# Two gate products called earlier, one lead for PSUM banks and operands in the planner, a new table of shifts and a new order of the first loads, in a float32 encoder block

## The chip, the cores and the metric

The kernel runs on one core of one Trainium2 chip. The metric is the device time of one execution in microseconds (us), lower is better; a kernel is timed in several runs and the median is given. TensorE is called PE here, VectorE DVE, ScalarE ACT, GpSimd POOL and the engine that issues most DMAs SP, as in the profile.

## What is computed

One layer of an encoder on 512 real tokens and 16 meta tokens of width 1024. The input is normalised, projected once, and goes through two attention mixers side by side; their results are gated per channel, merged and projected, and a gated feed-forward net follows. Cut to what matters:

```python
u = rms_norm(h, pre_mix_gain)
qa, ka, va, qb, kb, vb, g = split(u @ w_in)
o_swa  = windowed_gqa_sink_attention(rope(qa), rope(ka), va, sink)   # 16 heads, band of 3 blocks + meta keys
o_diff = differential_attention(rope(qb), rope(kb), vb, lam)         # 8 heads, two softmaxes each, dense
gates  = sigmoid(g + b_gate)                                         # 2 x 1024 channels
merged = gates[:, :1024] * (o_swa @ w_branch_swa) + gates[:, 1024:] * (o_diff @ w_branch_diff)
h = h + rms_norm(merged @ w_out)
f = (silu(u2 @ w_gate) * (u2 @ w_up)) @ w_ffn_out                    # u2 = rms_norm(h)
out = h + rms_norm(f)
```

All is float32 in and out. A product of two float32 matrices is made of three matmuls on operands that are split into a rounded high part and a remaining low part (fp32r): high by high, high by low, low by high. So each weight and each activation needs a copy (the high part, on ACT) and a subtraction (the low part, on DVE or POOL) before PE can use it.

## The kernel before

Everything lies transposed: channels on the 128 partitions, tokens along the row. The stages are, in order of time:

1. **Start.** The transposed input is loaded in eight tiles of 128 channels (`x_load`, L412 to L415, on SP) and split into `xh` on ACT (L419) and `xl` on DVE (L420). The weights of the first key projection come in four pieces between them (`k_weights`, L425 to L432). The line that lists the order is L434: `x0 w0 x1 x2 w1 x3 x4 w2 x5 x6 w3 x7`. The piece `w0` is loaded and split in two halves, for the channel tiles 0 and 1. PE runs 41 small matmuls on zeros first (L402), then L474: for each channel tile twelve matmuls, high weight by `xh`, high weight by `xl`, low weight by `xh`. DVE, ACT, SP and PE run in the order in which the code stands there.
2. **Planned stretch** (about 20 to 500 us). From `v_swa` to the second last stage every step is not issued at once but handed to a planner, `Plan` (L117 to L256). A step has an engine, a duration, what it reads and writes, and a priority. `Plan.run` then plays the steps through with these durations: for each engine it looks which steps have their operands and a free buffer, and takes the one with the lowest due time (on PE the priority alone; on the others the ready time plus a slack). The order found that way is the order in which the instructions are issued, and on the chip each engine keeps to it. A step that waits for an operand from another engine is ready a lag after that (`lag`, L138: 0.27 us to PE, 0.036 to 0.092 us to ACT, DVE and POOL). A step that needs a fresh buffer or PSUM bank is ready 0.05 us after the bank was left, on all engines (L219). `SHIFT` (L127) is a table of numbers that moves the due time of single steps by hand.
3. What is planned: keys, values and queries of the banded attention (`k_swa`, `v_swa`, `q_swa`), its 16 blocks (`s_swa`: scores `Sw` L763 on two banks, mask and minimum on DVE L767, exponential on ACT L771, scaling on POOL L778; `t_swa`: transposes `tr` L813, split into `ah` and `al`, products into the one bank `O` L820), the first eight gate products (`gate`), the differential attention (`qk`, `vd`, `s_diff` with scores `Sd` L912 in one double bank, `t_diff` with `Od` L981 and L983), the branch products `b1`, the second eight gate products (`gate2`), and of the branch product `w_bd` the first two column tiles, but for their last step in the sum. Products into the three banks `pr` are what PE does between the steps of the attentions.
4. **After the plan.** The gates `z2` get their tanh on ACT (L1113), the last step of the two `w_bd` tiles is made, then the other six, the output projection, and the feed-forward net, none of which the change touches.

The seam between plan and rest matters here. The last head ends in `t_diff(7)`: its sum of squares on PE (`mp`, L995 and L996), then on ACT `v` (L999), logarithm and exponential (L1004, L1005) and a square (L1006), three steps on DVE (L1007, L1009, L1011), the high part `dh` on ACT (L1018) and the low part `dl` on DVE (L274). The last step (k = 7) of every `w_bd` tile reads that `dh` and `dl`. The eight tanhs stand behind the plan in the code and are tied only to the last exponential (L1005); a scheduler of the framework places them among ACT's last steps.

In the program of before the gate products are called in this order: gates 0 and 1 ahead of the blocks, gates 2, 3, 4 and 5 behind blocks 0, 1, 2 and 8 (line L1062), gates 6 and 7 behind `qk(0)`.

Of the kernel before, what the change touches and what calls it, by code (L numbers as in the profile page):

```python
# [22 lines left out]
KT = D // P  # L23
# [93 lines left out]
class Plan:  # L117
# [9 lines left out]
    SHIFT = (  # L127
# [8 lines left out]

# [56 lines left out]
    def run(self):  # L193
# [4 lines left out]
        while any(todo.values()):  # L198
            best = None
            for e, ks in todo.items():  # L200
                cand = []
                for k in ks:
# [11 lines left out]
                    for tag, n in need.items():  # L214
                        f = sorted(x for x in self.slots[tag] if x is not None)
                        if len(f) < n:
                            t = None
                            break
                        t = max(t, f[n - 1] + 0.05)  # L219
                    if t is None:  # L220
# [38 lines left out]
def encoder(ctx, tc, I, out, dbg=None):  # L259
# [165 lines left out]
    def k_weights(i):  # L425
        if i % 2 == 0:
            wK.append([wp.tile([P, 4, 2, P], dt, tag=t, name=t, bufs=RB) for t, dt in (("wr", F32), ("wh", F32R), ("wl", F32R))])
        w = [t[:, 2 * (i % 2):2 * (i % 2) + 2] for t in wK[-1]]
        src = I["w_k"][i].rearrange("p (k a c) -> p k a c", k=2, a=2)
        for ks in (slice(0, 1), slice(1, 2)) if i == 0 else (slice(0, 2),):  # L430
            sp.dma_start(out=w[0][:, ks], in_=src[:, ks])
            split(w[1][:, ks], w[2][:, ks], w[0][:, ks])  # L432

    for what in ("x0", "w0", "x1", "x2", "w1", "x3", "x4", "w2", "x5", "x6", "w3", "x7"):  # L434
        n = int(what[1])
        if what[0] == "w":
            k_weights(n)
        else:
            x_load(n)
            x_split(n)  # L440
# [110 lines left out]
    def weights(src, dep=()):  # L551
# [5 lines left out]
        e, eng, xfer = ("ACT", act, 2.0) if nfill[0] > 3 else ("SP", sp, 0.0)  # L557
        T(e, 0.38, lambda: eng.dma_start(out=wr.t, in_=src.rearrange("p (k c) -> p k c", k=KT)), w=[wr], dep=dep,
          prio=pr_, land=0.7, xfer=xfer)
        T("ACT", 1.05, lambda: act.copy(out=wh.t, in_=wr.t), r=[wr], w=[wh], prio=pr_)  # L560
        if nfill[0] % 2:
            parts = []
            for q in range(4):
                ks = slice(2 * q, 2 * q + 2)
                parts.append(T("POOL", 0.69, lambda ks=ks: sub_hi(wl.t[:, ks], wr.t[:, ks], wh.t[:, ks], pool), r=[wr, wh],
                               keep=[wl], prio=pr_))
        else:
            parts = [T("DVE", 1.23, lambda: sub_hi(wl.t, wr.t, wh.t), r=[wr, wh], keep=[wl], prio=pr_, port=True)] * 4
# [43 lines left out]
    def move(out, in_, r, w, xfer, dep=()):  # L612
        return T("SP", 0.64, lambda: sp.dma_start(out=out().bitcast(F32), in_=in_().bitcast(F32)), r=r, w=w, dep=dep,
                 prio=2, xfer=xfer)
# [83 lines left out]
    def keys(n):  # L698
        K = buf("kk")
        K.mk = lambda: KP[(K.slot + 1) % 4][:, :, 0:n]  # L700
        return K
# [81 lines left out]
    def t_swa(u):  # L783
# [24 lines left out]
        for n, (o, kb) in enumerate(keys):  # L808
            tr = bank("tr", 2, "tr")

            def trans(o=o, tr=tr):
                for hh in range(4):
                    pe.transpose(out=tr.t[:, hh * P:(hh + 1) * P], in_=pt.t[:, hh, o:o + P], identity=ident)  # L813
            Ttr[u].append(T("PE", 0.355, trans, r=ph, w=[tr], keep=[pt], prio=0, chain="tr", land=0.08))
            ah, al = sb("ah", [P, 512], F32R, "ah", 2), sb("al", [P, 512], F32R, "al", 2)
# [79 lines left out]
    def s_diff(h):  # L895
# [9 lines left out]
        for c in range(2):  # L905
            for i in range(4):
# [16 lines left out]
                if c:  # L923
                    T("ACT", 0.2, lambda one=one: act.activation(out=den.t[:, 1, one], in_=den.t[:, 1, one], func=AF.Copy,
                                                                 scale=ilam), w=pw, on=["lam"], prio=0)
# [30 lines left out]
    def t_diff(h):  # L956
# [4 lines left out]
        for kb in range(5):  # L961
# [4 lines left out]
            def trans(o=o, kk=kk, tr=tr):  # L966
                for i in range(4):
                    pe.transpose(out=tr.t[0:kk, i * P:(i + 1) * P], in_=a[i]()[:, o:o + kk], identity=ident)  # L968
            T("PE", 0.355, trans, r=A, w=[tr], keep=hd["keep"], prio=0, chain="tr", land=0.08)
            if kb == 4:  # L970
# [86 lines left out]
    for u in range(16):  # L1057
        s_swa(u)
        t_swa(u)
        if u in (1, 5):  # L1060
            q_swa(2 + u // 4)
        for j in {0: (2,), 1: (3,), 2: (4,), 8: (5,)}.get(u, ()):  # L1062
            gate(j)
# [4 lines left out]
    qk(0)  # L1068
    for j in (6, 7):
        gate(j)  # L1070
    vd(0)
# [600 lines left out]
```

## Time and profile before

| what | us |
|---|---|
| median of three runs | 942.48 (941.61 to 942.53) |
| the profiled execution | 942.37 |
| its span, first to last instruction | 940.6 |
| PE busy | 928.5 |
| DVE, ACT, POOL busy | 714.9, 534.7, 253.5 |

The profiled execution took 942.37 us, 1.8 us of it outside the span of the instructions. PE has 5,852 matmuls. A matmul's record lasts longer than the distance to the next one: one of 512 columns is recorded with 0.39 us while the next starts about 0.23 us later, since they are pipelined and their ends are modelled. So PE can be shown as busy while it waits for up to some 0.16 us, and short waits are to be read from the distance of the starts. The granted clock of PE is 1.00 in every stretch up to 920 us.

### The profile page before, as it was taken

What the parts mean: (1) busy time and instruction counts of PE and PEld (TensorE: products, weight loads), DVE (VectorE), ACT (ScalarE), POOL (GpSimd) and SP (SyncE); (2) the same over time, 40 slices, a digit from 0 to 9 for tenths busy, and PEclk for the clock granted to TensorE, in tenths of its full rate; (3) what the DMA queues carried; (4) which work ended last, traced back from release to release, by engine and by line L of the source; (5) the groups of instructions that cost most, each with busy time, mean ns of one, the idle gap of its engine ahead of it and who ended that gap; (6) DMA issues with size and microseconds to landing.
All of it is one profiled execution on the core that took longest, in us unless ns stands there. A gap on an engine that the chain in (4) does not pass through costs nothing.

```text
span 940.6 us, 15671 instructions
## 1 busy us (share of the span) xinstructions
PE 928.5 (99%) x5852; PEld 831.9 (88%) x5852; DVE 714.9 (76%) x1194; ACT 534.7 (57%) x997; POOL 253.5 (27%) x320
## 2 busy tenths in 40 slices
PE   9999999999999999999999999999999999999996
PEld 9878878898898999999788888998999999988885
DVE  5847799997675767888664866876888888699975
ACT  6427677765565457667556433754555555555541
POOL 2645555564243333255032411500000000000000
PEclk9999999999999999999999999999999999999999
DMA  9564131216414333335332560364333333180122
GB/s 329 170 168 136 49 95 43 71 38 183 119 38 133 92 93 111 81 102 136 102 134 67 181 201 24 118 195 138 111 91 113 113 90 113 49 332 23 46 68 90
DMA packets 38012, 107.75 MB, mean 115 GB/s; under 512 B 6176, under 2 KB 7200, under 8 KB 37936
## 3 DMA queue, kind: packets, MB, share of 16 engines
q1 hardware_dynamic: 29872, 77.78, 27.7%
q10 hardware_dynamic: 8064, 28.97, 9.9%
q8 instruction: 46, 0.75, 0.3%
q14 instruction: 30, 0.25, 0.1%
HBM read 88.09 MB, written 2.10 MB: 96 GB/s over the span
## 4 chain that ended last, share of the span: by engine, by line
PE 88%; DVE 6%; ACT 2%; DMA 2%; issue 1%; SPq 0%; ACTq 0%; DVEq 0%
PE pr L308 20%; PE pr L310 20%; PE pr L309 20%; PE Sd L912 3%; PE wk L309 2%; PE wk L308 2%; PE wk L310 2%; PE tr L968 2%; PE O L820 2%; PE tr L310 1%; PE tr L308 1%; PE tr L309 1%; PE Od L981 1%; PE tr L813 1%; PE Sw L763 1%; DVE p L767 1%
## 5 line engine op out<-in xcount | busy, mean ns | idle before, releaser
L308 PE MATMUL pr<-xh,wh 128*128 128x264 f32 (+1 forms) x592 | 192.9, 326 | 0.4 <-DVE tb L585 0.2
L309 PE MATMUL pr<-xl,wh 128*128 128x264 f32 (+1 forms) x592 | 189.4, 320 | 0.0
L310 PE MATMUL pr<-xh,wl 128*128 128x264 f32 (+1 forms) x592 | 189.3, 320 | 0.0
L274 POOL TENSOR_TENSOR wl<-wr,wh 128x256 fp32r<-128x256 f32 (+1 forms) x130 | 126.8, 999 | 131.5 <-ACT wh L560 65.4
L308 PEld LDWEIGHTS pr<-xh,wh 128*128 128x128 f32 x592 | 111.4, 188 | 8.4 <-issue 0.5
L310 PEld LDWEIGHTS pr<-xh,wl 128*128 128x128 f32 x592 | 111.4, 188 | 8.4
L309 PEld LDWEIGHTS pr<-xl,wh 128*128 128x128 f32 x592 | 111.4, 188 | 7.8
L330 POOL TENSOR_TENSOR r3y<-r3v,mhalf 128x1 f32<-128x1 f32 x4 | 2.2, 551 | 321.6 <-DVE r3v L329 321.6
L274 DVE TENSOR_TENSOR wl<-wr,wh 128x1024 fp32r<-128x1024 f32 (+2 forms) x59 | 72.0, 1221 | 11.4 <-ACT wh L293 5.5
L560 ACT CAST wh<-wr 128x1024 fp32r<-128x1024 f32 x58 | 60.5, 1047 | 27.2 <-PE pr L309 24.3
L308 PE MATMUL pr<-TM,sx 128*128 128x256 f32 x236 | 66.9, 283 | 0.3 <-ACT s L1454 0.3
L309 PE MATMUL pr<-TM,sx 128*128 128x256 f32 x236 | 66.8, 283 | 0.0
L310 PE MATMUL pr<-TM,sx 128*128 128x256 f32 x236 | 66.8, 283 | 0.0
L274 DVE TENSOR_TENSOR sx<-S,sx 128x1024 fp32r<-128x1024 f32 x34 | 41.7, 1225 | 24.9 <-PE pr L309 12.7
L917 DVE TENSOR_REDUCE nm<-Sd 128x1 f32<-128x528 f32 x64 | 45.0, 704 | 20.4 <-PE Sd L912 19.8
L603 POOL TENSOR_TENSOR ta<-ta,tb 128x528 f32<-128x528 f32 (+1 forms) x26 | 39.1, 1505 | 60.8 <-DVE tb L585 56.2
L310 PE MATMUL pr<-uh,wl 128*128 128x256 f32 (+1 forms) x188 | 55.0, 293 | 0.1
L308 PE MATMUL pr<-uh,wh 128*128 128x256 f32 (+1 forms) x188 | 55.1, 293 | 0.0
L309 PE MATMUL pr<-ul,wh 128*128 128x256 f32 (+1 forms) x188 | 54.9, 292 | 0.0
L278 ACT CAST sx<-S 128x1024 fp32r<-128x1024 f32 x34 | 35.8, 1052 | 25.1 <-PE pr L310 8.1
L778 POOL TENSOR_SCALAR p<-p,rc 128x272 f32<-128x272 f32 (+1 forms) x64 | 38.5, 615 | 39.9 <-DVE rc L776 39.5
L308 PEld LDWEIGHTS pr<-TM,sx 128*128 128x128 f32 x236 | 45.3, 192 | 0.5 <-ACT s L1454 0.5
(528 smaller groups left out, 2650.0 us busy)
## 6 DMA issues: line engine op xcount, KB each, us to landing
wr<-in_w_in_dram ACTq DMA_DIRECT2D x45, 512.0 KB, 4.0
wg<-in_w_fi_dram SPq DMA_DIRECT2D x17, 512.0 KB, 3.6
wu<-in_w_fi_dram SPq DMA_DIRECT2D x17, 512.0 KB, 3.5
wr<-in_w_fi_dram SPq DMA_DIRECT2D x16, 512.0 KB, 3.6
b<-in_w_fo_dram SPq DMA_DIRECT2D x16, 512.0 KB, 9.2
KP<-hl SPq DMA_DIRECT2D x32, 132.0 KB, 2.5
Q<-hl SPq DMA_DIRECT2D x64, 64.0 KB, 2.0
Qd<-hl SPq DMA_DIRECT2D x64, 64.0 KB, 2.1
```

The lines of the kernel that those rows point to most:

```text
L274: (eng or dve).tensor_tensor(out=lo, in0=src, in1=hi.bitcast(F32), op=ALU.subtract)
L278: act.copy(out=hi, in_=src)
L308: pe.matmul(out=ps, lhsT=ah, rhs=bh, start=first, stop=False, **more)
L309: pe.matmul(out=ps, lhsT=ah, rhs=bl, start=False, stop=False, **more)
L310: pe.matmul(out=ps, lhsT=al, rhs=bh, start=False, stop=last, **more)
L560: T("ACT", 1.05, lambda: act.copy(out=wh.t, in_=wr.t), r=[wr], w=[wh], prio=pr_)
L603: T("POOL", 0.05 + 1.3 * m, lambda: pool.tensor_tensor(out=ta.t[:, :, 0:n], in0=ta.t[:, :, 0:n], in1=tb.t[:, :, 0:n], op=ALU.add), r=[tb], ...
L778: T("POOL", 0.22 + 0.41 * c, lambda z=z: pool.tensor_scalar(out=pt.t[:, z, 0:nk], in0=pt.t[:, z, 0:nk], scalar1=rc.t[:, z:z + 1], scalar2=1.0,
L820: T("PE", 0.232, lambda a=a, x=x, n=n, kb=kb: pe.matmul(out=O.t, lhsT=VS[g // 2].t[:, kb, g % 2].rearrange("p a b -> p (a b)"), rhs=a.t, s ...
L912: pe.matmul(out=S.t[:, s, 0:HALF], lhsT=Q[c].t[:, i * P:(i + 1) * P], rhs=K[c].t[:, x, s * HALF:(s + 1) * HALF], start=(x == 0), stop=(x = ...
L917: T("DVE", 0.71, lambda S=S, c=c, one=one: dve.tensor_reduce(out=nm.t[:, c, one], in_=S.t[:, :, 0:HALF], axis=AX.XY, op=ALU.min), r=[S], w ...
L968: pe.transpose(out=tr.t[0:kk, i * P:(i + 1) * P], in_=a[i]()[:, o:o + kk], identity=ident)
```

## The change

Five edits, all in the start and the planned stretch:

- The order of the first loads and splits: the channel tile `x1` is fetched and split ahead of the second half of `w0`, and the high part of that half is now made by a copy on DVE in place of ACT.
- In the planner a buffer that a PE step needs is taken as free 0.27 us after it was left (0.05 before), the same lead as for operands; other engines keep 0.05.
- Some durations: DMA issue on ACT 0.35 (0.38), on SP for moves 0.60 (0.64), a weight's subtraction on POOL 0.74 (0.69), four transposes on PE 0.40 (0.355), a small scaling on ACT 0.295 (0.20).
- The key buffers are taken with an offset of 3 in place of 1 in the ring of four.
- The gates 5, 6 and 7 are called behind blocks 5, 8 and 11 (before: gate 5 behind block 8, gates 6 and 7 behind `qk(0)`), and the table of shifts is a new one with 159 entries in place of 78.

```diff
     SHIFT = (
-        "39:2.27 71:16 98:-0.25 104:2.63 115:8 178:78 217:6 226:0.81 242:-8 251:2 262:0.35 290:-0.48 292:3.44 "
...
+        "48:-4.57 72:14 89:9.46 90:1.46 92:7.28 98:8.41 192:-3 216:-60 220:-3.87 226:-3.68 245:-133 254:-2 282:26 "
...
-                        t = max(t, f[n - 1] + 0.05)
+                        t = max(t, f[n - 1] + (0.27 if e == "PE" else 0.05))
...
-        for ks in (slice(0, 1), slice(1, 2)) if i == 0 else (slice(0, 2),):
-            sp.dma_start(out=w[0][:, ks], in_=src[:, ks])
-            split(w[1][:, ks], w[2][:, ks], w[0][:, ks])
-
-    for what in ("x0", "w0", "x1", "x2", "w1", "x3", "x4", "w2", "x5", "x6", "w3", "x7"):
+        if i == 0:
+            sp.dma_start(out=w[0][:, 0], in_=src[:, 0])
+            split(w[1][:, 0], w[2][:, 0], w[0][:, 0])
+            x_load(1)
+            sp.dma_start(out=w[0][:, 1], in_=src[:, 1])
+            x_split(1)
+            dve.tensor_copy(out=w[1][:, 1], in_=w[0][:, 1])
+            sub_hi(w[2][:, 1], w[0][:, 1], w[1][:, 1])
+            return
+        sp.dma_start(out=w[0], in_=src)
+        split(w[1], w[2], w[0])
+
+    for what in ("x0", "w0", "x2", "w1", "x3", "x4", "w2", "x5", "x6", "w3", "x7"):
...
-        T(e, 0.38, lambda: eng.dma_start(out=wr.t, in_=src.rearrange("p (k c) -> p k c", k=KT)), w=[wr], dep=dep,
+        T(e, 0.35, lambda: eng.dma_start(out=wr.t, in_=src.rearrange("p (k c) -> p k c", k=KT)), w=[wr], dep=dep,
...
-                parts.append(T("POOL", 0.69, lambda ks=ks: sub_hi(wl.t[:, ks], wr.t[:, ks], wh.t[:, ks], pool), r=[wr, wh],
+                parts.append(T("POOL", 0.74, lambda ks=ks: sub_hi(wl.t[:, ks], wr.t[:, ks], wh.t[:, ks], pool), r=[wr, wh],
...
-        return T("SP", 0.64, lambda: sp.dma_start(out=out().bitcast(F32), in_=in_().bitcast(F32)), r=r, w=w, dep=dep,
+        return T("SP", 0.6, lambda: sp.dma_start(out=out().bitcast(F32), in_=in_().bitcast(F32)), r=r, w=w, dep=dep,
...
-        K.mk = lambda: KP[(K.slot + 1) % 4][:, :, 0:n]
+        K.mk = lambda: KP[(K.slot + 3) % 4][:, :, 0:n]
...
-            Ttr[u].append(T("PE", 0.355, trans, r=ph, w=[tr], keep=[pt], prio=0, chain="tr", land=0.08))
+            Ttr[u].append(T("PE", 0.4, trans, r=ph, w=[tr], keep=[pt], prio=0, chain="tr", land=0.08))
...
-                    T("ACT", 0.2, lambda one=one: act.activation(out=den.t[:, 1, one], in_=den.t[:, 1, one], func=AF.Copy,
+                    T("ACT", 0.295, lambda one=one: act.activation(out=den.t[:, 1, one], in_=den.t[:, 1, one], func=AF.Copy,
...
-            T("PE", 0.355, trans, r=A, w=[tr], keep=hd["keep"], prio=0, chain="tr", land=0.08)
+            T("PE", 0.4, trans, r=A, w=[tr], keep=hd["keep"], prio=0, chain="tr", land=0.08)
...
-        for j in {0: (2,), 1: (3,), 2: (4,), 8: (5,)}.get(u, ()):
+        for j in {0: (2,), 1: (3,), 2: (4,), 5: (5,), 8: (6,), 11: (7,)}.get(u, ()):
             gate(j)
...
     qk(0)
-    for j in (6, 7):
-        gate(j)
     vd(0)
```

PE gets the same matmuls in another order. Three places of the order of the built programs follow; the line numbers of the changed program are 6 higher at the start and 12 to 14 higher in the plan.

The first place is the start, on DVE: the rows from the first split of an input tile on, of before. `xl` is the low part of an input tile, `wl` that of a key weight.

```order
L420 SCALAR_TENSOR_TENSOR xl<-xr,vec,xh 128x528
L274 TENSOR_TENSOR wl<-wr,wh 128x256 x2
L420 SCALAR_TENSOR_TENSOR xl<-xr,vec,xh 128x528 x2
L274 TENSOR_TENSOR wl<-wr,wh 128x512
L420 SCALAR_TENSOR_TENSOR xl<-xr,vec,xh 128x528 x2
L274 TENSOR_TENSOR wl<-wr,wh 128x512
```

The same of the changed program:

```order
L426 SCALAR_TENSOR_TENSOR xl<-xr,vec,xh 128x528
L280 TENSOR_TENSOR wl<-wr,wh 128x256
L426 SCALAR_TENSOR_TENSOR xl<-xr,vec,xh 128x528
L442 CAST wh<-wr 128x256
L280 TENSOR_TENSOR wl<-wr,wh 128x256
L426 SCALAR_TENSOR_TENSOR xl<-xr,vec,xh 128x528
L280 TENSOR_TENSOR wl<-wr,wh 128x512
```

The second half of the first weight piece now stands behind the low part of `x1`, and its high part (`CAST wh`) is on this engine too.

The second place is the seam, on ACT: the rows around the last head's `v`, of before. `z_5893`, `z_5595` and `z_5789` are the gates `z2` at their tanh, the `y` rows the logarithm and the exponential, `z<-y` the square, `wh<-wr` a weight's high part.

```order
L999 ACTIVATE v<-mp,epsc 128x512
L1004 ACTIVATE y<-v 128x512
L560 CAST wh<-wr 128x1024
L1005 ACTIVATE y<-y 128x512
L1113 ACT_TABLE_LOAD
L1113 ACTIVATE z_5893<-z_5893,hb 128x512 x3
L1113 ACTIVATE z_5595<-z_5595,hb 128x512 x2
L1113 ACTIVATE z_5789<-z_5789,hb 128x512 x2
L1006 ACTIVATE z<-y 128x512
L293 CAST wh<-wr 128x1024
L1018 CAST dh<-ob 128x512
L1113 ACTIVATE z_5893<-z_5893,hb 128x512
```

The same of the changed program:

```order
L299 CAST wh<-wr 128x1024
L1013 ACTIVATE v<-mp,epsc 128x512
L1018 ACTIVATE y<-v 128x512
L1019 ACTIVATE y<-y 128x512
L1125 ACT_TABLE_LOAD
L1125 ACTIVATE z_5822<-z_5822,hb 128x512 x4
L1125 ACTIVATE z_5601<-z_5601,hb 128x512 x2
L1125 ACTIVATE z_5755<-z_5755,hb 128x512 x2
L1020 ACTIVATE z<-y 128x512
L1032 CAST dh<-ob 128x512
```

All eight tanhs now stand between the exponential and the square, where seven stood; two weight casts left the chain.

The third place is the same seam, on PE: the rows around the last sum of squares `mp`, of before.

```order
L309 MATMUL pr<-xl,wh 128x512
L310 MATMUL pr<-xh,wl 128x512
L995 MATMUL mp<-sh,ones 128x512
L996 MATMUL mp<-sl,ones 128x512
L308 MATMUL pr<-xh,wh 128x512
```

The same of the changed program:

```order
L315 MATMUL pr<-dl,wh 128x512
L316 MATMUL pr<-dh,wl 128x512
L1009 MATMUL mp<-sh,ones 128x512
L1010 MATMUL mp<-sl,ones 128x512
L314 MATMUL pr<-dh,wh 128x512
```

Before, 69 product rows of 512 columns follow `mp` up to the first matmul that reads the last head (the k = 7 step of `w_bd` tile 0): 27 of gate products (operands `xh`, `xl`) and 42 of the two `w_bd` tiles (operands `dh`, `dl`). In the changed program the gate products are all ahead of `mp`, three rows of `w_bd` as well, and 39 rows follow. Those 39 are all `w_bd` products of the first seven heads.

20 rows, old and new, of the table SHIFT are left out of this document.

## The prediction

> **What bounds the kernel now.** I read the page first, for the engines:
>
> ```profile
> span 940.6 us, 15671 instructions
> PE 928.5 (99%) x5852; PEld 831.9 (88%) x5852; DVE 714.9 (76%) x1194; ACT 534.7 (57%) x997; POOL 253.5 (27%) x320
> ```
>
> PE is the bound, and the change gives it the same 5,852 matmuls. So only time in which PE waits can be won or lost. Then busy time by stretch (columns after the stretch: PE, weight load, DVE, ACT, POOL), once for the stages of the plan and once in steps of 20 us:
>
> ```profile
> 60.00:220.00 160.00, 158.14 (x913) 134.35 (x913) 135.54 (x363) 107.95 (x268) 83.55 (x135) 1.00 0.30 85
> 220.00:440.00 220.00, 219.93 (x1547) 203.82 (x1546) 160.74 (x277) 135.80 (x282) 88.02 (x95) 1.00 0.37 103
> 440.00:500.00 60.00, 59.54 (x305) 49.07 (x305) 37.87 (x64) 35.76 (x70) 19.44 (x23) 1.00 0.41 119
> ```
>
> ```profile
> 160.00:180.00 20.00, 19.80 (x127) 17.46 (x126) 19.22 (x54) 13.86 (x38) 10.87 (x17) 1.00 0.22 54
> ```
>
> The banded attention (60 to 220) shows 1.86 us of idle PE, the differential attention (220 to 500) 0.53. In the middle of the banded attention DVE is busy for 19.22 of 20 us, more than anywhere else in the plan. The waits of PE name few culprits:
>
> ```profile
> PE O L820 <- DVE ot L832: 0.6, 2, 0.5
> PE tr L968 <- DVE dal L274: 0.4, 1, 0.4
> PE Sw L763 <- DVE nm L767: 0.2, 1, 0.2
> ```
>
> Most waits are too short to show, since a record overlaps the next one. They are in the distances of the starts. The timeline of PE, from the first matmul of 60 to 500 us to the last of the 2,765 (913 + 1547 + 305), with one place between:
>
> ```profile
> 60.06 0.40 PE L309 MATMUL pr<-xl,wh 128*128 128x512 f32 x1
> ...
> 338.96 0.70 PE L912 MATMUL Sd<-KP,Qd 128*128 128x264 f32 x4
> 339.50 0.28 PE L308 MATMUL pr<-xh,wh 128*128 128x264 f32 x1
> 339.62 0.28 PE L309 MATMUL pr<-xl,wh 128*128 128x264 f32 x1
> ...
> 341.32 0.71 PE L912 MATMUL Sd<-KP,Qd 128*128 128x264 f32 x4
> ...
> 343.70 0.72 PE L912 MATMUL Sd<-KP,Qd 128*128 128x264 f32 x4
> ...
> 499.90 0.39 PE L310 MATMUL pr<-xh,wl 128*128 128x512 f32 x1
> ```
>
> Undisturbed, the next start follows 0.121 us after a matmul of 264 columns, 0.125 of 272, 0.182 of 400, 0.229 of 512; four transposes cost 0.35 and 0.085 more in the matmul behind them. Every excess over that of more than 0.02 us, summed over these rows: 7.5 us in 60 to 220, 3.9 in 220 to 500, **11.4 us in all**. That is the most that better planning can win.
>
> **The change part by part.** The sums are made on the profiled execution, 942.37 us; it lies 0.1 under the median of 942.48.
>
> *The start.* Rows of the chain of waits, and of ACT, DVE and PE:
>
> ```profile
> 2.58 4.58 DMA xr<-in_xT_dram
> ```
>
> ```profile
> 6.51 0.41 ACT L278 CAST wh<-wr 128x256 fp32r<-128x256 f32 x1 [1.53 <-DMA wr<-in_w_k_dram]
> 6.95 0.43 DVE L274 TENSOR_TENSOR wl<-wr,wh 128x256 fp32r<-128x256 f32 x1 [1.13 <-ACT wh L278]
> 7.18 1.36 ACT L419 ACTIVATE xh<-xr,vec 128x528 fp32r<-128x528 f32 x2 [0.26 <-DMA xr<-in_xT_dram]
> 7.95 1.45 DVE L420 SCALAR_TENSOR_TENSOR xl<-xr,vec,xh 128x528 fp32r<-128x528 f32 x2 [0.58 <-ACT xh L419]
> 7.97 0.63 PE L474 MATMUL pr<-xh,wh 128*128 128x264 f32 x3 [0.54 <-ACT xh L419]
> 9.86 0.54 PE L474 MATMUL pr<-xh,wh 128*128 128x264 f32 x3
> ```
>
> ```profile
> L514 DVE COPY rb<-r0y 128x128 f32<-128x128 f32 x4 | 0.6, 224 | 0.0
> ```
>
> The half weight landed at 6.51, `x1` (264 KB) at 7.16, so `x1` behind half the bytes comes at about 6.84 (bounds 6.51 and 7.16). Then 0.74 for `xh` on ACT, and 0.03 + 0.78 for `xl` on DVE: 8.39. Only behind that, on the same engine, stands the new copy, and PE's first matmul on `x1` needs it. No row shows such a copy; 0.22 (128 columns, above) and 0.43 (the subtraction of the same tile) bound it, and I take 0.30, between both. PE starts at 8.7 in place of 7.97, but `xl` is ready then, so the twelve matmuls run through in 1.46 + 0.1: the next tile starts at 10.3 in place of 9.86. **+0.4** (0 to +0.9). `x1` gets earlier, but its partner gets later.
>
> *Banks with the lead of operands.* Sd has one double bank; the next group may start when DVE (`nm`) and ACT (exponential) are through with the last. The groups at 338.96, 341.32 and 343.70 are 2.36 and 2.38 apart, where the 19 matmuls from one to the next need 19 x 0.121 = 2.30: PE waits 0.06 to 0.08 each time, and no row shows it as idle. In the order of before 12 of the 63 distances hold 2.16 to 2.30 us of matmuls, and these 12 waited 1.1 us together; in the new order none holds less than 2.54. At 2.54 seven of eight groups waited for nothing (of five at 2.55, between 233 and 245 us, three did wait). **-1.1** (-0.8 to -1.5).
>
> *The banded attention, 7.5 us of waits.* The order shows more cover for banks: from a group of four transposes to the next but one, which takes its bank, at least 2.58 us of matmuls (2.01 before); from the last product into `O` to the next block's first at least 1.98 (1.75). It shows none for operands: from transposes to the product on `ah` at least 1.09 (1.14), on `al` 1.75 (1.83). And more than half of the 7.5 us lies where DVE is full, as at 160 to 180, where the cover didn't decide. So I take 40%: **-3.0**. Bounds: +1.0 (waits move, and denser neighbours make new ones) and -6.0 (four fifths go).
>
> *The gates.* The text of the change says that two gates move into the banded attention. They are there already:
>
> ```profile
> L844 DVE TENSOR_TENSOR t<-pr,rbc x8: 669/686/692, 51.0 to 186.4; 128x512 f32<-128x512 f32 x8
> ```
>
> ```profile
> L763 PE MATMUL Sw<-KP,Q x128: 282/342/450, 74.8 to 201.7; 128*128 128x400 f32 x64, 128*128 128x272 f32 x64
> ```
>
> All eight gate products end between 51.0 and 186.4, the scores of the bands run from 74.8 to 201.7. What moves is their place among the blocks, by some 20 us, and with each its DMA issue and cast on ACT, its subtraction on POOL or DVE and its product and tanh: the same work in the same stretch. **0** by itself, inside the bounds above.
>
> *The rest of the differential attention, 3.9 - 1.1 = 2.8 us.* The largest piece is the wait on `dal` above. The new durations are nearer to the rows (ACT's small scaling, POOL's subtraction), so a quarter goes: **-0.7** (+0.5 to -2.0). The offset in the key buffers only follows the new order of the ring: 0. A move's shorter duration may bring keys and queries later than planned by some tenths, but the scores stand 16 us of matmuls or more behind the last product that feeds them, in both orders: 0.
>
> *The seam after the plan.* Nothing in the diff speaks of it, but the two orders do. Rows of PE, ACT and DVE at the last head:
>
> ```profile
> 497.10 0.40 PE L996 MATMUL mp<-sl,ones 128*128 128x512 f32 x1
> ```
>
> ```profile
> 497.54 0.69 ACT L999 ACTIVATE v<-mp,epsc 128x512 f32<-128x512 f32 x1 [2.58 <-PE mp L996]
> 498.26 0.63 ACT L1004 ACTIVATE y<-v 128x512 f32<-128x512 f32 x1
> ...
> 499.74 0.63 ACT L1005 ACTIVATE y<-y 128x512 f32<-128x512 f32 x1
> 500.38 1.28 ACT L1113 ACT_TABLE_LOAD   x1
> 501.68 4.41 ACT L1113 ACTIVATE z<-z,hb 128x512 f32<-128x512 f32 x7
> 505.99 0.62 ACT L1006 ACTIVATE z<-y 128x512 f32<-128x512 f32 x1
> ...
> 509.89 0.62 ACT L1018 CAST dh<-ob 128x512 fp32r<-128x512 f32 x1 [2.34 <-DVE ob L1011]
> ```
>
> ```profile
> 506.64 0.69 DVE L1007 SCALAR_TENSOR_TENSOR z<-z,v 128x512 f32<-128x512 f32 x1 [5.50 <-ACT z L1006]
> 507.37 0.69 DVE L1009 SCALAR_TENSOR_TENSOR y<-z,y 128x512 f32<-128x512 f32 x1
> ...
> 509.11 0.75 DVE L1011 SCALAR_TENSOR_TENSOR ob<-ob,g,y 128x512 f32<-128x512 f32 x1
> ...
> 510.55 0.69 DVE L274 TENSOR_TENSOR dl<-ob,dh 128x512 fp32r<-128x512 f32 x1
> ```
>
> Before, `dl` is done 14.1 us after `mp` (511.24 - 497.10), and the 69 matmuls behind `mp` cover 69 x 0.2275 = 15.7: no wait. Now 39 matmuls follow; the first that reads `dh` could start 40 x 0.2275 = 9.1 after `mp`. The new chain, from starts of the rows: 0.44 to `v`, 0.72, 0.64 (no cast between now), 0.64 to the table load, 1.30 to the tanhs, eight of them at 4.31 / 7 = 0.616, that is 4.93, 0.65 to DVE, 0.73, 0.73 (no weight between), 0.78 to `dh` and 0.62 for it: 12.2. PE waits 3.1. Its second matmul there needs `dl`, at 0.66 + 0.69 after the start of `dh`: 12.9, another 0.5, and 0.1 for the weights not loaded ahead. **+3.7** (3.0, if two handovers run into each other, to 4.5). PE issues in order, so the products of tile 2 behind it cannot fill the gap, and the ones ahead are used up.
>
> The Trainium skill would price the table load higher: ScalarE: Activation LUTs, section "What ACT_TABLE_LOAD costs", gives 1283 ns for the load and about 1380 ns for a drain, 2.66 us per switch. By that rule the seam would cost 5.1 and the total be 1.4 higher. The row has the load's 1.28, but the first tanh starts 1.30 after the load's start, so no run here shows the drain as time between the two, and the row is used.
>
> Sum: 942.37 + 0.4 - 1.1 - 3.0 - 0.7 + 3.7 = **941.7 us**.
>
> **The rivals.** (1) *The waits go almost all.* Bank lead and the new table take 8 of the 11.4 us. For it: the cover rose for every kind of bank. Against: the cover for `ah` and `al` didn't, and DVE is as full. 942.37 + 0.4 - 8.0 + 3.7 = 938.5. (2) *The seam costs nothing*, because ACT gets through earlier than I add up. Against: eight tanhs and the load alone are 6.2 of the 9.1 us, and they stand ahead of the square. 942.37 + 0.4 - 4.8 = 938.0. (3) *Slower: the seam stays and DVE keeps the waits of the banded attention.* The place is 100 to 220 us: DVE's queue at 19.2 of 20 us sets when banks and operands come, whatever PE does between, so the 7.5 us stay. 942.37 + 0.4 - 1.1 - 0.7 + 3.7 = 944.7, and 945.7 with 1.0 of new waits. It decides as soon as that stretch wins less than 0.3. (4) *The change does not do what it says*: so it is for the gates, and it is in the forecast at 0.
>
> **How the numbers follow.** A measurement of this kernel can tell about 0.2%, 1.9 us, from no change: faster is under 940.6, slower over 944.4. The forecast, a gain of four to six us in the attentions with some 4 us of it given back at the seam, has a chance of 0.52, and its own range is 940.6 to 943.8. Rival 1 has 0.24, rival 2 0.08, rival 3 0.16. Hence 0.32, 0.52, 0.16. The range takes in rival 1 and 2 to 938.0 and rival 3 to 945.0.
>
> **What would show it.** In the profile after: PE idle 3 to 4 us in one place, in front of the k = 7 product of `w_bd`, released by ACT's `dh`, with eight tanhs in one row ahead of it; between 220 and 440 us no two Sd groups under 2.5 apart; the next tile of the start at about 10.3. The forecast is wrong if no idle stands at that seam, or if the sum of the start distances over 60 to 220 still holds 7 us, or under 2.

## The result, and the profile after

The changed kernel takes 951.03 us (median of five runs, 949.33 to 951.41) beside 942.06 (941.18 to 942.53) of the kernel before on the same chip: **1.0094 times the time, 95% interval 1.0079 to 1.0108**. It is slower by 9 us, outside the range and on the side to which the prediction gave the least. The profiled execution took 951.29 us.

The first lines of its page:

```profile
span 949.5 us, 15686 instructions
PE 930.4 (98%) x5852; PEld 833.6 (88%) x5852; DVE 715.0 (75%) x1195; ACT 537.2 (57%) x996; POOL 247.7 (26%) x320
```

PE has the same 5,852 matmuls; the span is 8.9 us longer. The stretches of before that the prediction showed, and the seam (PE, weight load, DVE, ACT, POOL, clock, DMA):

```profile
60.00:220.00 160.00, 156.38 (x890) 131.56 (x889) 138.53 (x363) 107.95 (x269) 81.53 (x136) 1.00 0.32 91
160.00:180.00 20.00, 19.47 (x130) 17.25 (x131) 18.95 (x54) 13.04 (x34) 10.21 (x17) 1.00 0.22 54
220.00:440.00 220.00, 217.70 (x1531) 202.83 (x1532) 155.91 (x268) 132.64 (x272) 81.74 (x89) 0.99 0.35 97
440.00:500.00 60.00, 60.00 (x325) 51.10 (x325) 40.61 (x69) 35.79 (x73) 21.94 (x27) 1.00 0.45 128
500.00:520.00 20.00, 17.50 (x79) 13.92 (x77) 7.34 (x9) 13.94 (x21) 0.00 (x0) 1.00 0.17 53
```

PE gets through 890 matmuls in the banded stretch where it got through 913, and there are two places of 2 us and more in which it stands still. PE's longest waits name them:

```profile
PE pr L314 <- ACT dh L1032: 3.0, 1, 3.0
PE Sd L926 <- DMA Qd<-hl: 2.1, 1, 2.1
PE O L834 <- DVE ot L846: 1.3, 3, 0.5
```

Short waits don't show there, so I summed the excess of PE's start distances again, by the same pitches as in the prediction (us, more than 0.02 each, one profiled execution of each kernel):

| stretch | before | after | predicted change | measured |
|---|---|---|---|---|
| 0 to 60, the start | 1.6 | 2.1 | +0.4 | +0.5 |
| 60 to 220, banded attention | 7.5 | 10.3 | -3.0 | **+2.9** |
| 220 to 500, differential attention | 3.9 | 5.1 | -1.8 | +1.2 |
| 500 to 540, the seam | 0.0 | 5.1 | +3.7 | +5.1 |
| behind 540 | 2.2 | 2.5 | 0 | +0.3 |

The sum of the waits grew by 9.8 us, the span by 8.9. Such a sum can differ by 0.8 us from one execution to another: E12 below, with the planned order of before, has 3.1 in 220 to 500. Three places carry the loss.

**The seam.** PE around the last sum of squares `mp`, then ACT (start, duration):

```profile
508.24 0.39 PE L1010 MATMUL mp<-sl,ones 128*128 128x512 f32 x1
...
517.12 0.39 PE L316 MATMUL pr<-dh,wl 128*128 128x512 f32 x1
520.49 0.67 PE L314 MATMUL pr<-dh,wh 128*128 128x512 f32 x1 [2.99 <-ACT dh L1032]
521.22 0.80 PE L315 MATMUL pr<-dl,wh 128*128 128x512 f32 x1
521.81 0.63 PE L316 MATMUL pr<-dh,wl 128*128 128x512 f32 x1
522.24 0.63 PE L314 MATMUL pr<-dh,wh 128*128 128x512 f32 x1
```

```profile
508.67 0.69 ACT L1013 ACTIVATE v<-mp,epsc 128x512 f32<-128x512 f32 x1 [0.33 <-PE mp L1010]
...
510.71 1.28 ACT L1125 ACT_TABLE_LOAD   x1
512.00 5.03 ACT L1125 ACTIVATE z<-z,hb 128x512 f32<-128x512 f32 x8
516.93 0.62 ACT L1020 ACTIVATE z<-y 128x512 f32<-128x512 f32 x1
519.82 0.62 ACT L1032 CAST dh<-ob 128x512 fp32r<-128x512 f32 x1 [2.27 <-DVE ob L1025]
```

This is what the prediction described: eight tanhs in one row ahead of the square, `dh` done 12.2 us after `mp` (520.44 - 508.24), a wait of 3.15 us (3.37 from start to start, less 0.23), then 0.50 and 0.37 for `dl` and the weights. What it did not have is in the last two rows: the matmuls behind the gap are 0.43 us apart in place of 0.23, until 523.9. The granted clock ahead of the gap and behind it:

```profile
515.00:520.00 5.00, 2.50 (x12) 1.73 (x10) 2.14 (x3) 2.73 (x6) 0.00 (x0) 1.00 0.00 0
520.00:525.00 5.00, 4.46 (x12) 3.21 (x13) 3.21 (x4) 2.53 (x3) 1.78 (x1) 0.66 0.00 0
```

The clock was halved for 3.4 us, which cost another 1.1 us. The Trainium skill has this: TensorE: Matmul & The Clock Gate, section "Part 1: The HAM clock gate", puts the array at half clock after an idle window of about 3.4 us and counts in windows that run on freely. Its 426.7 ns for 512 columns at half clock agrees with the 0.43 here; the idle here was 3.0 us by the row.

**A wait on a query.** PE at the first scores `Sd` of a head, ACT's and PE's rows, and the chain of waits:

```profile
397.89 0.28 PE L316 MATMUL pr<-xh,wl 128*128 128x264 f32 x1
400.28 0.73 PE L926 MATMUL Sd<-KP,Qd 128*128 128x264 f32 x4 [2.10 <-DMA Qd<-hl]
```

```profile
394.97 0.33 ACTq L572 DMA_DIRECT2D wr<-in_w_in_dram  x1
```

```profile
394.61 0.59 SPq L627
...
395.25 4.89 DMA Qd<-hl
```

The move of the query was issued at 395.25 and landed after 4.9 us; the median of such moves around it is 2.0. A weight load of 512 KB had been issued on ACT's queue 0.3 us ahead of it. PE lost 2.26 us here, and behind it ran at a clock of 0.66 (400 to 405 us), which cost 1.3 of the 1.7 us of excess there; 0.3 is a wait of the next `Sd`.

**The banded attention.** DVE's rows at one of the waits for `O`, with PE's after them:

```profile
102.02 0.50 DVE L781 CUSTOM_DVE_ANT_0 p<-Sw,mk,nsink 128x272 f32<-128x272 f32 x1
...
102.44 0.69 DVE L280 TENSOR_TENSOR al<-tr,ah 128x512 fp32r<-128x512 f32 x1
103.04 0.41 DVE L846 TENSOR_TENSOR ot<-O,ot 64x256 f32<-64x256 f32 x1
...
104.67 0.34 DVE L818 SCALAR_TENSOR_TENSOR aTm<-tr,vec,ma 32x128 fp32r<-32x128 f32 x1
105.03 0.50 DVE L781 CUSTOM_DVE_ANT_0 p<-Sw,mk,nsink 128x272 f32<-128x272 f32 x1
...
105.56 0.35 DVE L818 SCALAR_TENSOR_TENSOR aTm<-tr,vec,ma 32x128 fp32r<-32x128 f32 x1
105.93 0.69 DVE L280 TENSOR_TENSOR al<-tr,ah 128x512 fp32r<-128x512 f32 x1
```

```profile
105.94 0.40 PE L316 MATMUL pr<-xh,wl 128*128 128x512 f32 x1
106.68 0.50 PE L834 MATMUL O<-al,Vs 128*128 128x512 f32 x1 [0.35 <-DVE al L280]
```

`al` ends at 106.62 and PE goes on at 106.68. DVE itself stood still for no more than some 0.04 us between any two steps from 103.67 on; PE waits for a queue. And the rows show a thing that I had read past. Between steps on all 128 partitions the next one starts some 0.08 us before the last one's end (102.02 + 0.50 against 102.44; 102.44 + 0.69 against 103.04). At the steps on 32 or 64 partitions it starts 0.01 to 0.04 after the end (105.56 against 105.53, 105.93 against 105.91). From 60 to 215 us, of the 107 steps of DVE that start on other partitions than the step ahead of them 106 did so; of the 179 others 135 overlapped, 31 came after an idle DVE and 13 did not overlap. The Trainium skill has the rule: VectorE: DVE Perf Modes, section "Two Vector instructions with no wait between them", gives as a model that a step whose input or output starts in another group of 32 partitions than the last one's starts only when all earlier steps have finished. The trace agrees in 106 of 107.

The planner takes 0.083 us of overlap for every step of DVE (the table `OVER`), so it is wrong by about 0.105 us at each of the 106: 11 us. Set against the trace, PE's steps fall behind the planner's own times by 10.3 us in the banded stretch of before (27.1 to 37.5 us from the planned start) and by 11.9 after (27.3 to 39.2). Theory D, from here on: **DVE sets the pace of the bands, later than either of the two plans knows, and PE waits for it.** The rival, B: the waits come from banks and the order of PE's steps, as the prediction had it.

The same sum, taken by the product in front of which PE waits, speaks for D. In 60 to 220 us the waits in front of the scores `Sw`, which need a bank, fell from 1.8 to 0.7 us, as the new lead should make them; those in front of the products into `O` rose from 2.7 to 5.8, and those in front of the transposes `tr` from 1.4 to 3.0.

### The profile page after: what moved, and what is told of

The parts are those of the page before. It is cut to its first block, busy times and chain, and to the rows that moved or that the text cites. A ratio compares the mean times of both kernels' runs of the same rounds, so it can differ in the third digit from the quotient of the medians.

```text
span 949.5 us, 15686 instructions
## 1 busy us (share of the span) xinstructions
PE 930.4 (98%) x5852; PEld 833.6 (88%) x5852; DVE 715.0 (75%) x1195; ACT 537.2 (57%) x996; POOL 247.7 (26%) x320
## 4 chain that ended last, share of the span: by engine, by line
PE 82%; DVE 7%; ACT 4%; DMA 3%; issue 2%; SPq 1%; POOL 0%; DVEq 0%; ACTq 0%; POOLq 0%
PE pr L316 19%; PE pr L315 19%; PE pr L314 19%; PE Sd L926 3%; PE wk L315 2%; PE wk L314 2%; PE wk L316 2%; PE tr L982 2%; PE tr L315 1%; PE tr L314 1%; PE tr L316 1%; PE Od L995 1%; PE O L834 1%; PE Sw L777 1%; DMA xr<-in_xT_dram 1%
## 5 line engine op out<-in xcount | busy, mean ns | idle before, releaser
L617 POOL TENSOR_TENSOR ta<-ta,tb 128x528 f32<-128x528 f32 (+1 forms) x26 | 36.2, 1394 | 57.6 <-DVE tb L599 57.3
L792 POOL TENSOR_SCALAR p<-p,rc 128x400 f32<-128x400 f32 (+1 forms) x64 | 36.2, 580 | 43.2 <-DVE rc L790 43.1
L785 ACT ACTIVATE p<-p,nm 128x273 f32<-128x273 f32 (+1 forms) x64 | 36.9, 577 | 17.9 <-DVE nm L781 17.3
```

Of the source, the lines that this page charges most:

```text
L617: T("POOL", 0.05 + 1.3 * m, lambda: pool.tensor_tensor(out=ta.t[:, :, 0:n], in0=ta.t[:, :, 0:n], in1=tb.t[:, :, 0:n], op=ALU.add), r=[tb], ...
L785: T("ACT", 0.38 + 0.34 * c, lambda hh=hh: act.activation(out=pt.t[:, hh, 0:nk + 1], in_=pt.t[:, hh, 0:nk + 1], func=AF.Exp, scale=-1.0, bi ...
L792: T("POOL", 0.22 + 0.41 * c, lambda z=z: pool.tensor_scalar(out=pt.t[:, z, 0:nk], in0=pt.t[:, z, 0:nk], scalar1=rc.t[:, z:z + 1], scalar2=1.0,
```

## The experiments

All times are medians of 4 to 11 runs, on one chip for those of one group; before stood at 941.5 to 941.9 beside them. Ratios are to before. Waits are sums of PE's start distances, as in the table, of one execution each.

**E1: the tanhs behind the last `dh`** (changed kernel).

```diff
-            act.copy(out=dd[0][:, h, :], in_=ob.t)
+            hix.append(act.copy(out=dd[0][:, h, :], in_=ob.t))
...
-        behind(act.activation(out=z2[j], in_=z2[j], func=AF.Tanh, scale=0.5, bias=hb[:, 8 + j:9 + j]), lnx[-1:])
+        behind(act.activation(out=z2[j], in_=z2[j], func=AF.Tanh, scale=0.5, bias=hb[:, 8 + j:9 + j]), hix[-1:])
```

> The changed kernel with one edit: the eight tanhs of the gates z2 are tied behind the last head's dh in place of its exponential. Theory S (the seam costs what ACT's tanhs and table load put ahead of the square): the chain from the last sum of squares to dh loses 6.2 us (1.28 + 5.03 less the handover), dh is done some 7 us after that sum where 39 products cover 9.1 us, so the wait of 3.1 us on dh and the 1.9 us of short waits behind it go: 4 to 5 us faster, near 946.5. Rival (the tanhs are needed as soon as dh, by the products that take z2, so the wait only moves to the first tiles behind): less than 1.5 us faster, and a new wait on DVE or ACT shows up within 20 us behind the seam.

Measured: 944.64 us, ratio 1.0035 (1.0022 to 1.0049), 6.4 us under the changed kernel. ACT's rows:

```profile
509.06 0.63 ACT L1020 ACTIVATE z<-y 128x512 f32<-128x512 f32 x1
511.97 0.62 ACT L1032 CAST dh<-ob 128x512 fp32r<-128x512 f32 x1 [2.27 <-DVE ob L1025]
512.61 1.28 ACT L1125 ACT_TABLE_LOAD   x1
513.90 5.02 ACT L1125 ACTIVATE z<-z,hb 128x512 f32<-128x512 f32 x8
```

No distance of PE's starts is longer than its pitch between 500 and 540 us: the 5.1 us are gone and nothing took their place. The other 1.3 of the 6.4 us lie elsewhere: the waits of 220 to 500 us are 3.9 here, 5.1 in the changed kernel's trace. The wait on the query is still there (2.66 us in this execution), but the clock held behind it:

```profile
400.00:405.00 5.00, 4.79 (x34) 4.40 (x35) 2.78 (x5) 3.29 (x6) 2.19 (x4) 1.00 0.00 0
```

An idle PE of 2.1 us lost the clock in one execution, one of 2.5 us did not in another. What decides it was not tried.

**E2: one weight load later** (changed kernel; the planner's order is kept, one step is held back).

```diff
-            k.fn()
+            k.n == 2314 or k.fn(), k.n == 2226 and self.tasks[2314].fn()
```

> The changed kernel with one edit: one DMA issue on ACT, the 512 KB weight load at 394.97 us, is issued behind the two casts that stand after it, some 3.5 us later. Theory Q (that load shares the DMA engines with the last two moves of a head's queries, which landed after 4.9 us in place of 2.0): the move lands near 397.3, the scores Sd at 397.9 do not wait, the 2.26 us there and the 0.34 behind go: 2.0 to 2.6 us faster, near 948.7. Rival (the move is late by its own queue: twelve moves on SP, each 0.6 us, behind a low part made 8 us earlier): the wait stays over 1.5 us and the time within 0.7 us of the changed kernel.

Measured: 949.00 us, ratio 1.0075 (1.0062 to 1.0087), 2.0 us under the changed kernel. PE at the same place:

```profile
397.29 0.28 PE L316 MATMUL pr<-xh,wl 128*128 128x264 f32 x1
397.58 0.73 PE L926 MATMUL Sd<-KP,Qd 128*128 128x264 f32 x4
```

The wait is 0.17 us, and no move of the queries took over 3.1 us (4.9 before). Theory Q holds: the two transfers got into each other's way. The waits of 220 to 500 us fell by 2.9; this execution lost 1.2 more at the seam, where the clock stayed halved for 6 us.

**E3 and E4: half of the small steps left out**, in the changed kernel and in the one before.

```diff
-                T("DVE", 0.35, lambda rs=rs, cs=cs: dve.scalar_tensor_tensor(
+                T("DVE", 0.35, lambda rs=rs, cs=cs, hh=hh: hh % 2 or dve.scalar_tensor_tensor(
```

> The changed kernel without 32 of its 64 small DVE steps in the banded attention (the low part of the meta keys' weights for two of four heads in each block is left out, so part of the result is not computed); the order of all else is the same. 32 x 0.35 us = 11.2 us of DVE work less in 80 to 220 us. Theory D (DVE sets the pace of the blocks, PE waits for it): the waits of PE in 60 to 220 us fall from 10.3 to 5 or less, the kernel is 5 to 9 us faster. Rival B (banks and the order of PE's steps make the waits, DVE is only busy): the waits fall by less than 1.5 us and the time too.

> The kernel of before without the same 32 small DVE steps (same part of the result left out). Theory D: its waits in 60 to 220 us fall from 7.5 to under 4, the kernel is 3 to 6 us faster, and most of the difference between the two kernels in that stretch (2.9 us) is gone. Rival B: less than 1.5 us faster, and the difference stays.

Measured: 942.78 (ratio 1.0008, 0.9999 to 1.0017), 8.2 us under the changed kernel (of it 6.5 in the bands and 1.8 in 220 to 500, by the waits), and 937.89 (0.9959, 0.9947 to 0.9972), 4.0 under before. The banded stretch of E3, then of E4:

```profile
60.00:220.00 160.00, 159.14 (x943) 138.46 (x941) 132.58 (x342) 112.41 (x279) 86.69 (x141) 1.00 0.32 91
```

```profile
60.00:220.00 160.00, 159.23 (x945) 138.34 (x945) 125.75 (x336) 110.08 (x273) 86.73 (x140) 1.00 0.31 88
```

PE gets through 943 and 945 matmuls where it had 890 and 913. The waits fell from 10.3 to 3.8 us and from 7.5 to 3.7: with less DVE work the two orders are equal. That is theory D; rival B, with its bound of 1.5 us, falls. It doesn't show which step of the new order makes DVE cost PE 2.9 us more than before.

**E5, E6, E7: single edits on the kernel before.** E5 calls the gates as the change does and renumbers the old table; E6 has the lead alone; E7 the six durations alone. E6 and E7 have E1's edit, so that the seam doesn't stand in them.

```diff
-        for j in {0: (2,), 1: (3,), 2: (4,), 8: (5,)}.get(u, ()):
+        for j in {0: (2,), 1: (3,), 2: (4,), 5: (5,), 8: (6,), 11: (7,)}.get(u, ()):
...
-                        t = max(t, f[n - 1] + 0.05)
+                        t = max(t, f[n - 1] + (0.27 if e == "PE" else 0.05))
```

> The kernel of before with one edit: gates 5, 6 and 7 called behind blocks 5, 8 and 11, and its own old table of shifts carried over step by step to the new numbers of the steps. As the prediction had it, the place of the gates is worth 0: 942 us within 1, waits in 60 to 220 us 7.5 within 1. Rival G (the weights' low parts of two more gates fall to DVE and POOL while the blocks need DVE): the waits there go to 10 or more and the kernel is 2 to 4 us slower. The seam keeps its 69 products behind the last sum of squares in this order, so no wait is expected there in either case.

> The kernel of before with the lead of 0.27 us for banks and its old table; the tanhs are tied behind the last dh, since only 48 products cover the seam in this order. As the prediction had it: the waits of scores Sd fall from 2.8 to about 1, those of the bands' scores Sw from 1.8 to about 0.7, PE's other waits stay: 1 to 3 us faster. Rival (DVE sets the pace, and an old table fits no new plan): the banks' waits go but come back as waits for operands in 60 to 220 us, 942 within 1 or slower.

> The kernel of before with the six new durations alone, old table, the tanhs tied behind the last dh (42 products cover the seam). The prediction put the new durations at a gain of under 0.7: 941 to 942.5. Rival (any change of the plan's numbers makes another order that the old table doesn't fit): 2 to 5 us slower, spread over the whole planned stretch.

Measured: gates 943.37 us (ratio 1.0021, 1.0012 to 1.0029), lead 960.05 (1.0197, 1.0183 to 1.0211), durations 947.51 (1.0070, 1.0057 to 1.0083). The gates cost 1.9 us, and the waits rose by as much in the banded stretch (7.5 to 9.3, of it 180 to 200 us from 1.5 to 3.2): more than the 0 of the prediction, less than rival G's 2 to 4. The durations made the kernel 6.0 us slower, more than the rival's 2 to 5. The lead made it 18.6 us slower, beyond both expectations, with 17 us of waits between 220 and 260 us:

```profile
PE Sd L912 <- ACT pp L920: 5.8, 3, 2.4
PE O L820 <- ACT ah L649: 2.2, 2, 1.5
```

This says little of the lead: the planner's own sum of waits of PE is 5.3 us with before's numbers and table, 25 with the new lead and the old table (7.0 in E7, 7.9 in E5), and 3.9 in the changed kernel. A table of shifts belongs to the numbers it was made for, so no edit of the plan can be priced alone this way, the 1.9 us of the gates included. And by the planner's own sum the change was a gain of 1.4 us; on the chip it was none. The offset in the key buffers was not tried.

**E8: E1 and E2 together** (changed kernel).

> The changed kernel with both mends: the tanhs behind the last dh, and the one weight load behind the two casts. If the two losses are independent: 951.0 - 6.4 - 2.0 = 942.6, less if the second wait had also lost clock (1.4 of the 1.7 us behind it are at half clock). What is then left against before is the banded stretch (10.3 against 7.5 us of waits) less the bank waits that went: 941.5 to 943.5. Rival: under 940, then the order of the bands is no loss.

Measured: 943.36 us, ratio 1.0018 (1.0009 to 1.0028), within the 941.5 to 943.5. The waits are 0 at the seam, 2.3 in 220 to 500 (3.9 before, 3.1 in E12) and 10.3 in the bands (7.5 before). So the plan did gain in the differential attention, 0.8 to 1.6 us, and the bands take more than that back.

**E9, E10: a plan with the missing rule, and its control.** The kernel before with E1's edit, the lead, the new durations, transposes at 0.44, 2.0 us from a move to PE (0.77), 0.30 (0.27) from the other engines to PE, and a step on other partitions than the last one later by 0.105 (ACT 0.1). For these numbers the table was searched anew (2,072 entries) against the planner's own waits. E10 is the same with the rule's two numbers at 0, and its own search.

```diff
+    def turn(k, quad):
+        return {"DVE": 0.105, "ACT": 0.1}.get(k.eng, 0.0) if k.q != quad.get(k.eng, 0) else 0.0
...
-                    cand.append((max(t, free[e], port + 0.02 * (holder == e) if k.port else 0.0), due, k))
+                    cand.append((max(t, free[e] + self.turn(k, quad), port + 0.02 * (holder == e) if k.port else 0.0), due, k))
...
-                    op1=ALU.subtract), r=[tm, w], w=[D_], prio=1)
+                    op1=ALU.subtract), r=[tm, w], w=[D_], prio=1, q=hh)
```

> The kernel of before, planned anew: tanhs behind the last dh, lead 0.27 for banks, the new durations, four transposes at 0.44, 2.0 us from a move to PE, and one rule that neither kernel's planner has: on DVE and ACT a step that starts on other partitions than the step ahead of it starts 0.105 us later (0.1 on ACT). For these numbers a new table of shifts was searched until the planner itself showed 0.3 us of waits of PE. Theory D (the planner's missing rule makes DVE late on the chip, by about 106 such steps x 0.105 = 11 us between 60 and 215 us, and PE waits for it): the plan now holds on the chip, the waits in 60 to 220 us fall from 7.5 to under 3, those in 220 to 500 to under 2: 932 to 937 us. Rival (what PE waits for are the chip's deviations from any plan, and a table that is searched harder is fitted harder to the plan alone): 940 or slower.

> As the kernel planned anew, but with that one rule off (its two numbers at 0), and a table searched for that until the planner itself showed 0.7 us of waits. Theory D: the plan looks as good as the other one's but doesn't hold, DVE falls behind by about 9 us in the banded attention, where the waits of PE stay at 6 us or more: 5 to 10 us slower than the kernel with the rule. Rival: within 2 us of it.

Measured: E9 937.59 us (ratio 0.9956, 0.9944 to 0.9969), E10 940.22 (0.9985, 0.9976 to 0.9994). Between the two lie 2.6 us, not the 5 to 10 expected and not within the rival's 2; E9 misses its 932 to 937 by 0.6. The waits in the bands are 5.7 and 8.1. Set against the plan, DVE's steps fall behind from 80 to 220 us by 10.2 us before, by 9.0 in E10 and by 6.3 in E9: the rule explains some 2.7 of the lag, not all of it. Each of the two has one search of its own, and the planned waits differ by 0.4 us (0.7 and 0.3); how far two searches for the same numbers differ was not tried.

Over half of E9's 5.7 us are two waits of 1.36 and 1.62, both ahead of a first product into `O`. At the second DVE's lag stays within 0.4 us from 152 to 161 us, and then grows by 2.1 at once. ACT's rows there, then DVE's and PE's:

```profile
161.04 0.37 ACT L1014 COPY ot<-O 64x256 f32<-64x256 f32 x1 [4.11 <-DVE ol L458]
...
163.28 0.35 ACT L1014 COPY ot<-O 64x256 f32<-64x256 f32 x1
```

```profile
160.40 0.53 DVE L458 TENSOR_TENSOR ol<-ot,oh 128x256 fp32r<-128x256 f32 x1
...
163.66 0.85 DVE L1016 TENSOR_TENSOR ot<-O,ot 64x256 f32<-64x256 f32 x2 [2.13 <-ACT ot L1014]
```

```profile
162.81 0.40 PE L494 MATMUL pr<-xh,wl 128*128 128x512 f32 x1
164.66 0.47 PE L1004 MATMUL O<-ah,Vs 128*128 128x512 f32 x1 [1.45 <-DVE ot L1016]
```

ACT sat idle for 4.1 us until DVE had read an earlier block's `ot` (160.40 + 0.53). In the planner only the first of the two copies of a block asks for that buffer, and here the second had been put first: the plan held the buffer to be free. The same swap stands in three blocks of the order of before, in five of after, in eight of E9 and in seven of E10; what it costs in those of before and after was not tried.

**E11: the two copies in order**, the table searched anew (2,109 entries).

```diff
-            T("ACT", 0.38, lambda r=r, rs=rs: act.copy(out=ot.t[rs, 0], in_=Ov()[64:128, :, r, :]), r=[O], w=[tb_[r]],
-              keep=[ot], prio=-1, q=10 + r)
+            cp.append(T("ACT", 0.38, lambda r=r, rs=rs: act.copy(out=ot.t[rs, 0], in_=Ov()[64:128, :, r, :]), r=[O],
+                        w=[tb_[r]], keep=[ot], dep=cp[-1:], prio=-1, q=10 + r))
```

> The kernel planned anew with the rule of the quadrants, and one step more: the two ACT copies out of the bank O are kept in the order of the code. In the plan of the run before, the second copy of a block could stand ahead of the first, which alone asked for the buffer ot, so the chip waited for a buffer that the plan held to be free (1.36 and 1.62 us, both ahead of the first product into O). A new table, 0.4 us of planned waits. Theory D with this mend: the two waits go, the waits in 60 to 220 us fall from 5.7 to under 3.5: 933 to 936 us. Rival (the chip finds other waits of that size in any plan): 937 or slower.

Measured: **933.21 us, ratio 0.9908 (0.9895 to 0.9922)**, 8.5 us faster than before and some 18 faster than the changed kernel. The same stretches as above:

```profile
60.00:220.00 160.00, 159.52 (x956) 140.20 (x956) 139.03 (x370) 111.56 (x273) 85.46 (x143) 1.00 0.33 94
160.00:180.00 20.00, 20.00 (x146) 18.69 (x144) 19.20 (x56) 14.94 (x40) 9.67 (x18) 1.00 0.16 37
```

DVE is as busy as ever (19.2 of 20 us), and PE does 956 matmuls in place of 913: the waits in the bands are 2.0 us, those of 220 to 500 are 0.4. So DVE did not have too much to do for PE: there is an order in which the same work costs PE little. From 80 to 220 us DVE now falls behind its plan by 3.1 us (10.2 before). The rule's share of the 8.5 us is the 2.6 between E10 and E9; the rest is shared by the mend, the other numbers of the plan and the searches. How much of E11's gain over E9 is the mend and how much the other search was not tried apart.

**E12: the start alone** (kernel before; the edit is that of the change).

> The kernel of before with the new order of the first loads and splits alone; the plan and its order are the same. The prediction's step: +0.4 us (0 to +0.9). By the traces of the two kernels the third tile of the start begins 0.15 us earlier: -0.1 to -0.3 us. Both lie within what a measurement can tell; the place of the third tile's first product (9.86 us before, 9.71 in the changed kernel) decides.

Measured: 942.10 us, ratio 1.0004 (0.9995 to 1.0013): no difference that can be told. The third tile's first product starts at 8.98 us (9.86 before), but PE then waits for the weights behind the first projection, PE and ACT:

```profile
24.67 0.39 PE L308 MATMUL pr<-xh,wh 128*128 128x264 f32 x1 [0.82 <-ACT wh L515]
```

```profile
24.00 1.14 ACT L515 CAST wh<-wr 128x512 fp32r<-128x512 f32 x2 [0.23 <-DMA wr<-in_w_in_dram]
```

In this trace what `x1` gains is lost to a later load; the DMA engines are 92% busy in the first 20 us here and before.

## Why the prediction was wrong, step by step

- **The banded attention, "So I take 40%: -3.0": this is the step that failed.** It measured +2.9 us. The argument counted matmuls that cover banks, and took a share of the waits for it, though it had itself seen that DVE was full. The waits for the banks of `Sw` did fall, by 1.1 us, but those for what DVE hands on rose by more. With half of DVE's small steps left out (E3, E4), 6.5 of the 10.3 us and 3.8 of the 7.5 go, and with them the whole difference between the kernels. That DVE was later than the plan stood in the rows of before already, in the small steps' starts; E9 and E10 give this rule 2.6 us. The bound was wrong too: +1.0 for "waits move", where 2.9 came. Which part of the new order makes the 2.9 stays open.
- **The gates, "0 by itself".** E5 has +1.9 with the old table, in the bands. "The same work in the same stretch" was no argument where DVE is full, and for DVE not quite true: in 60 to 220 us of the changed kernel it makes the low parts of eight weight tiles of 128x1024 (11.5 us), before of seven (8.8). What that costs was not tried.
- **A move's duration and the scores, "16 us of matmuls or more ... 0".** 17 us lie between the last product for that head and its `Sd`, and they were not enough: twelve moves on SP take 8 us, the last low part came late on DVE, and the last move met a weight load. 3.6 us with the clock in the changed kernel's trace. The step counted cover, but not the chain it had to cover. That it was the load is shown (E2); the new duration of a move was not tried by itself.
- **The seam, +3.7: right.** `dh` at 12.2 and `dl` at 12.9 us came out as forecast, E1 shows the cause; 5.1 in all, since 1.1 us of halved clock and 0.3 at the handover were missing.
- **Sd's bank and the rest, -1.1 and -0.7: right in sign and near in size.** No two groups between 220 and 440 us are under 2.5 us apart (in before 12 are). With the query's wait mended (E8) the waits of `Sd` fell from 2.8 to 1.9 us, and all those of 220 to 500 from 3.9 (3.1 in E12) to 2.3, where 1.8 less was forecast.
- **The start, +0.4.** The waits up to 60 us rose by 0.5, though the third tile began at 9.71, not 10.3; E12 shows no effect on the time that can be told.
- **The rivals.** Number 3 named the mechanism, DVE's queue, and had a chance of 0.16; its price of 944.7 to 945.7 lacked the 2.9, the query's wait and the clock. Numbers 1 and 2 did not occur.

## What to carry to other kernels

Before counting cover in an order, set the planner's own times against the trace and see on which engine it falls behind: here one rule of DVE that the planner lacked was worth 2.6 us, and a buffer that it held to be free stood behind two of the longest waits that were left. A table fitted harder to numbers that lack the rule left the waits on DVE as they were (8.1 us in E10, 7.5 before), though it won 1.5 us in all. A plan's end says nothing of the work behind it (the tanhs at the seam) and little of transfers that run at the same time, so both have to be followed by hand. Where PE waits for 2 us or more, reckon with the halved clock behind the wait: here it cost 1.1 to 2.3 us where it came.

## What the runs showed of the hardware

- A DVE step on another group of partitions than the one ahead starts about 0.105 us later than its neighbours on the same partitions do: 0.01 to 0.04 us after the end of the one ahead, in place of 0.08 before it (106 of 107 such steps from 60 to 215 us). ACT's two copies of a block from `O`, on 64 partitions each, show the like: their starts are 0.38 apart, and each lasts 0.37.
- Behind idle PE of 3.0 us at the seam the matmuls of 512 columns came every 0.43 us for 3.4 us (6 us in E2); behind 2.1 us of idle the clock fell once, behind 2.5 us it did not.
- A move of 64 KB landed after 4.9 us in place of 2.0 when a load of 512 KB had been issued on another queue 0.3 us ahead.
- Eight tanhs start 1.29 us after the table load and it records 1.28: no further time lies between the two.
